# A hybrid decoder step on one core: another order for the steps of its token mixing

## The chip, the cores and the metric

The kernel runs on one core of one Trainium2 chip. The metric is the device time of one execution in microseconds (us); less is better. Three timed runs of the kernel before gave 1505.63, 1511.18 and 1495.79 us, the median is 1505.63 us.

## The reference

One inference step of a one-layer decoder, for 512 prompt tokens and 8 x 8 sample tokens (576 columns in all) with a model width of 1024, in float32. Cut to what matters:

```
x = x + 0.5 * swiglu(rmsnorm(x), ffn1)
z = rmsnorm(x) @ w_in                       # zs (RWKV), zc (conv), zq (attention), zg (gates)
y_a = rwkv7(zs)                             # 8 heads of 64: shift, decay, wkv scan, group norm
y_b = silu(layernorm(depthwise_conv31(glu(zc)))) @ w_conv_out
y_c = attention(zq, 256 memory tokens) @ w_xattn_out
g0, g1, g2 = sigmoid(zg)
x = x + (g0 * y_a + g1 * y_b + g2 * y_c) @ w_o
x = x + 0.5 * swiglu(rmsnorm(x), ffn2);  y = rmsnorm(x)
```

Beside y, the new RWKV states, shift rows, convolution tails and the memory's keys and values are outputs.

## The kernel before

Activations lie transposed, 128 channels in the partitions and 576 token columns in the free dimension, in two halves of 288. Every float32 matrix is split into a high and a low fp32r part, and a product is three matmuls (high by high, high by low, low by high). A **projection** (`proj`, line 111) loads one 128 x 1024 weight tile from HBM, splits it (ACT casts the high part at line 95, DVE subtracts the low part at line 96) and runs 8 x 3 matmuls for each half, 48 in all, at line 109, into two banks of the PSUM group `p`.

The first feed-forward layer, the token mixing and the second feed-forward layer follow one another. The mixing is what the change is about. Its steps are written down by hand in the string `PLAN` (line 28) and traced in that order by the loop at line 252:

- **A**: attention (770) to the memory, with two projections; results in `oc`.
- **P0 to P3**: preparation (866) of one pair of RWKV heads. Three projections with the token shift (`shifted`, 588) into the single tiles `k`, `r`, `v`; then a row of small passes through the PSUM group `g`: sums of squares (910), spreading of the norms (915), the products `gr` (945, 947), transposes (958 to 963).
- **I0 to I3**: inverse (1017) of the small triangular matrices of that pair, as a chain of 51 dependent DVE instructions (1045 to 1049). The data is laid out anew by way of HBM before it (1031, 1033, into the one tile `lt`) and after it (1053 to 1058, from the one tile `tt`): 14 DMAs on SP's queue.
- **J0 to J3**: joined (1060), two small rounds of matmuls that fill in the corner of the inverse.
- **B0 and B2**: the chains (966, 1109) of two pairs each, eight 64-token chunks in order, each a short sequence of PE, ACT and DVE steps, with the samples' chunk between them and `py` in group `g`; then `mixed` (974), group norm and gating of the result, for the first pair through group `c`, for the second through `g`. B0's result goes to HBM, B2's stays in SBUF for the merge.
- **G0**: the convolution's inputs (`glu`, 695), four projections. **C0**: the convolution itself (`conv`, 719), 124 DVE instructions (727 to 731), then a layer norm in three passes through group `g` (mean at 734, sums and root at 742, spreading at 746), SiLU, and the split into `cb` (751).
- **Y, X, Z**: gates, eight of each (848, 854). Y is a projection with a sigmoid and a store; X adds the attention's output projection from `oc` (12 matmuls); Z the convolution's from `cb` (12 matmuls) and adds to what X stored. The number behind the letter says how many.
- **L0**: reads the first two pairs' results back (1010).

Three things set the order in which the chip does this. First, the tile layer puts each engine's instructions into a fixed order at build time; it goes by the program's order, but takes an instruction of a later step where one of an earlier step would not be ready. Second, PSUM groups are rings: `p` has 3 banks, `g` 2 and `c` 3, and a ring is handed out in the program's order, so that a later step's `g` pass can't come before an earlier step's. The same holds for the weight tiles, so projections run strictly in the program's order: this row of projections is called the background stream below. Third, tiles that exist once (`k`, `r`, `v`, `lt`, `tt`) have to be free again. The tiles of the odd pairs and of the chains (`b21`, `b3`, with `vu`) are made when attention has given up its own.

Before the mixing's steps proper, `low_rank` (631) makes decay, mixing rate and gate for all four pairs; line 691 copies the gate's eight half tiles from PSUM.

Of the kernel before, what the change touches and what calls it, by code (L numbers as in the profile page):

```python
# [9 lines left out]
ALU = mybir.AluOpType  # L10
# [14 lines left out]
NORMED = 1  # L25

ROOMS = (8, 9, 10, 11, 12, 0, 1, 2, 3, 4, 8, 9, 10, 11, 5, 6, 7, 0, 8, 9, 10, 11)
PLAN = ("A0 P0 I0 Y3 G0 P1 J0 I1 Y3 X1 J1 B0 X3 P2 I2 Y2 X2 P3 J2 X2 I3 C0 Z2 J3 B2 Z4 L0 Z2")
PADN = 8 * 65 + 8 * 9
GRP = 11  # L30
NPROB = 36
# [18 lines left out]
class _Builder:  # L50
# [122 lines left out]
    def build(self):  # L173
        tc, a = self.tc, self.a
        with ExitStack() as st:
# [22 lines left out]
            with ExitStack() as sf:  # L198
# [17 lines left out]
                for k in range(8):  # L216
# [34 lines left out]
                    "Z": [(lambda i=i: self.gated(gp, 1, "cb", self.cb, i, 0)) for i in range(8)]}  # L251
            for step in PLAN.split():
                n = int(step[1:])
# [377 lines left out]
    def low_rank(self, zp):  # L631

        V, A, T, a, b1 = self.V, self.A, self.T, self.a, self.b1
        two = lambda name, n: zp.tile([128, 2, n], F32R, name=name)
        sub = lambda o, x, hi: V.tensor_tensor(o, x, hi.bitcast(F32), ALU.subtract)
        wh, wl, gh, gl = two("wh", 512), zp.tile([128, 512], F32R, name="wl"), two("gh", 512), zp.tile(
            [128, 512], F32R, name="gl")
        xs, lg, gs = two("xs", N), two("lg", N), zp.tile([128, N], F32R, name="gs")  # L640
        x = b1.tile([128, N], F32, name="k")
        self.shifted(12, x, b1)
        A.activation(x[:64], x[:64], AF.Tanh)
        for i in range(2):
            o, q = slice(64 * i, 64 * i + 64), slice(64 - 64 * i, 128 - 64 * i)
            A.copy(xs[o, i], x[o])
            sub(xs[q, i], x[o], xs[o, i])
        x = b1.tile([128, N], F32, name="r")
        self.shifted(13, x, b1)
        A.activation(x, x, AF.Sigmoid)  # L650
        self.split(lg[:, 0], lg[:, 1], x)
        x = b1.tile([128, N], F32, name="av")[:96]
        self.shifted(14, x, b1)
        A.activation(x, x, AF.Sigmoid)
        A.copy(gs[:96], x)
        sub(gs[32:64], x[32:64], gs[32:64])

        t = b1.tile([128, 1024], F32, name="lt")
        self.dma(t, a["wda"])
        t = t.rearrange("p (i c) -> p i c", i=2)  # L660
        A.copy(wh, t)
        for i in range(2):
            o = slice(64 * i, 64 * i + 64)
            sub(wl[o], t[o, i], wh[o, i])
        t = [b1.tile([128, PADN], F32, name=n)[:, :512] for n in ("w", "g")]
        for i in range(2):
            self.dma(t[i], a["wg"][:, 512 * i:512 * i + 512])
            A.copy(gh[:, i], t[i])
        sub(gl, t[0], gh[:, 0])
        sub(gh[64:96, 1], t[1][64:96], gh[64:96, 1])  # L670

        def products(*ops):
            for h in range(2):
                c = slice(h * H, (h + 1) * H)
                p = self.bank("g")[:, :H]
                for q, (l, r) in enumerate(ops):
                    T.matmul(p, l, r[:, c], start=q == 0, stop=q == len(ops) - 1)  # L677
                yield c, p

        for j in range(4):  # L680
            ch = slice(128 * j, 128 * j + 128)
            for i, (par, out, name) in enumerate((("w0", self.d_w, "bv"), ("a0", self.d_a, ("k", "r")[j % 2]))):
                t = b1.tile([128, N], F32, name=name, bufs=2 - i)
                o = slice(64 * i, 64 * i + 64)
                for c, p in products((wh[:, i, ch], xs[:, i]), (wl[o, ch], xs[o, i])):
                    A.activation(t[:, c], p, AF.Sigmoid, bias=self.par(par, j))
                self.store(out[j], t)
            t = b1.tile([128, N], F32, name=("av", "zt")[j % 2])
            for c, p in products((gh[:, 0, ch], lg[:, 0]), (gh[:, 0, ch], lg[:, 1]), (gl[:, ch], lg[:, 0]),
                                 (gh[:96, 1, ch], gs[:96])):  # L690
                A.copy(t[:, c], p)
            self.store(self.d_gt[j], t)


# [670 lines left out]
```

## Time and profile before

| | |
|---|---|
| timed runs | 1505.63, 1511.18, 1495.79 us |
| profiled execution, its own time | 1491.07 us |
| its span, first to last instruction | 1489.2 us |
| PE busy | 1449.4 us (97%) |
| DVE busy | 1028.1 us (69%) |
| ACT busy | 664.4 us (45%) |
| mean granted TensorE clock | 0.974 |
| mixing, from its first steps to the merge | about 430 to 1000 us from the span's start |

All times below that name a place ("at 644 us") count from the span's start. A row of the windows view gives, for a stretch from A to B: its length, then busy time and number of instructions of PE, PEld (weight loads), DVE, ACT and POOL, the granted TensorE clock, the DMA engines' share and GB/s. A row of the timeline gives start, length, engine, line, operation, tile written and tiles read, number of instructions, and in brackets the idle time before it with what ended it. A row of a source line gives the count, the shortest, median and longest duration in ns, and the first and last start. A row of the groups of instructions gives the count, the busy time in us, the mean of one in ns, and the engine's idle time before them. A PE that is called busy is not at its peak: its matmuls overlap.

### The profile page before, as it was taken

Reading aid. Unit: us, or ns where it says so; the run is one execution under the profiler, and the core shown is the slowest. Engines: PE = TensorE matmul, PEld = TensorE weight load, DVE = VectorE, ACT = ScalarE, POOL = GpSimd, SP = SyncE. Lnnn points to the kernel's source line nnn. Section 1 sums busy time; section 2 is a strip of 40 time slices with the busy share of each in tenths; the row PEclk is TensorE's granted clock in tenths of the full one; section 3 lists DMA queues with packets and bytes.
Section 4 is the critical chain, followed back from the end, with each engine's and each line's share of the span. In section 5 each row is a group of like instructions: output and inputs, shape, how many; then the busy total and the mean of one; then the engine's idle time right before and its main releaser. Section 6 shows DMA issues by size and latency. Waiting matters only on the chain.

```text
span 1489.2 us, 27301 instructions
## 1 busy us (share of the span) xinstructions
PE 1449.4 (97%) x10884; PEld 1384.6 (93%) x10884; DVE 1028.1 (69%) x2059; ACT 664.4 (45%) x1348; POOL 5.0 (0%) x22
## 2 busy tenths in 40 slices
PE   9999999999999999999999887999999999999998
PEld 9999999999988889899889786889999999999997
DVE  7976777777875629896347763348578767777775
ACT  7443444444577733534355422344444433444442
POOL 0000000000000000000000000000000000000000
PEclk9999999999999999999999877989999999999999
DMA  6222222323644143344122332227322322233221
GB/s 209 72 86 86 86 85 86 98 88 99 198 149 154 57 140 80 89 124 117 49 89 88 92 114 75 74 87 258 101 85 72 94 78 86 89 89 107 85 86 64
DMA packets 98444, 151.28 MB, mean 102 GB/s; under 512 B 43997, under 2 KB 53725, under 8 KB 98317
## 3 DMA queue, kind: packets, MB, share of 16 engines
q1 hardware_dynamic: 97740, 148.95, 32.2%
q8 instruction: 85, 1.39, 0.4%
q10 hardware_dynamic: 576, 0.59, 0.1%
q14 instruction: 43, 0.34, 0.1%
HBM read 130.03 MB, written 19.48 MB: 100 GB/s over the span
## 4 chain that ended last, share of the span: by engine, by line
PE 90%; DVE 6%; issue 1%; ACT 1%; DMA 1%; SPq 0%; DVEq 0%; POOL 0%; ACTq 0%; POOLq 0%
PE p L109 50%; PE p L384 26%; DVE pr L1045 2%; DVE tt L1047 1%; PE g L945 1%; DVE wl L96 1%; PE g L677 1%; PE c L1122 1%; PE g L1153 1%; PE c L1139 1%; PE g L137 1%; DVE cc L730 1%; PE c L1086 1%; PE g L147 1%; PE c L1132 1%
## 5 line engine op out<-in xcount | busy, mean ns | idle before, releaser
L109 PE MATMUL p<-x,wh 128*128 128x288 f32 x3136 | 653.7, 301 | 4.2 <-ACT wh L95 3.5
L109 PEld LDWEIGHTS p<-x,wh 128*128 128x128 f32 x3136 | 511.8, 191 | 12.4 <-ACT wh L95 4.2
L109 PE MATMUL p<-x,wl 128*128 128x288 f32 x1568 | 472.0, 302 | 6.8 <-DVE wl L96 6.7
L95 ACT CAST wh<-w 128x512 fp32r<-128x512 f32 (+1 forms) x354 | 210.3, 600 | 260.9 <-PE p L384 100.0
L109 PEld LDWEIGHTS p<-x,wl 128*128 128x128 f32 x1568 | 298.5, 191 | 12.9 <-DVE wl L96 8.7
L96 DVE TENSOR_TENSOR wl<-w,wh 128x512 fp32r<-128x512 f32 (+1 forms) x354 | 232.5, 662 | 109.8 <-ACT wh L95 99.5
L384 PE MATMUL p<-t,wh 128*128 128x288 f32 x1088 | 224.3, 299 | 0.0
L384 PEld LDWEIGHTS p<-t,wh 128*128 128x128 f32 x1088 | 173.9, 188 | 6.4 <-DVE t L395 6.4
L384 PE MATMUL p<-b,wh 128*128 128x288 f32 x816 | 169.7, 295 | 0.0
L384 PE MATMUL p<-t,wl 128*128 128x288 f32 x544 | 160.6, 295 | 0.0
L95 ACT CAST wh<-p 128x512 fp32r<-128x512 f32 x136 | 84.5, 621 | 155.9 <-PE p L109 117.4
L384 PEld LDWEIGHTS p<-b,wh 128*128 128x128 f32 x816 | 132.8, 188 | 0.0
L96 DVE TENSOR_TENSOR wl<-p,wh 128x512 fp32r<-128x512 f32 x136 | 93.6, 688 | 50.6 <-ACT wh L95 47.8
L384 PE MATMUL p<-b,wl 128*128 128x288 f32 x408 | 120.4, 295 | 0.0
L384 PEld LDWEIGHTS p<-t,wl 128*128 128x128 f32 x544 | 102.5, 188 | 0.0
L384 PEld LDWEIGHTS p<-b,wl 128*128 128x128 f32 x408 | 76.8, 188 | 0.0
L462 DVE SCALAR_TENSOR_TENSOR x<-p,x 128x288 f32<-128x288 f32 x128 | 57.8, 451 | 21.2 <-PE p L109 21.2
L95 ACT CAST x<-t 128x576 fp32r<-128x576 f32 (+1 forms) x60 | 36.5, 610 | 44.8 <-DVE t L466 42.2
L374 DVE TENSOR_TENSOR p<-w 128x512 f32<-128x512 f32 x68 | 46.7, 686 | 2.4 <-DMA w<-wu 2.0
L374 DVE TENSOR_TENSOR p<-p,w 128x512 f32<-128x512 f32 x68 | 46.4, 682 | 0.1
L851 ACT ACTIVATE gate<-p 128x288 f32<-128x288 f32 x48 | 19.7, 410 | 55.9 <-PE p L109 50.6
L1165 DVE SCALAR_TENSOR_TENSOR st<-c,gc,mg 64x64 f32<-64x64 f32 x56 | 15.8, 283 | 41.3 <-PE c L1143 28.9
(380 smaller groups left out, 1990.9 us busy)
## 6 DMA issues: line engine op xcount, KB each, us to landing
w<-wu SPq DMA_DIRECT2D x85, 512.0 KB
w<-win SPq DMA_DIRECT2D x44, 512.0 KB
w<-wd SPq DMA_DIRECT2D x64, 256.0 KB
w<-wd SPq DMA_DIRECT2D x16, 384.0 KB
d_mb<-gate SPq DMA_DIRECT2D x16, 288.0 KB
w<-wo SPq DMA_DIRECT2D x8, 512.0 KB
d_x<-x SPq DMA_DIRECT2D x16, 144.0 KB
d_g<-gate SPq DMA_DIRECT2D x8, 288.0 KB
```

The costliest lines, as they stand in the source:

```text
L95: self.A.copy(hi, x)
L96: self.V.tensor_tensor(lo, x, hi.bitcast(F32), ALU.subtract)
L109: self.T.matmul(p, l, x[r][:, c], start=k == 0 and i == 0, stop=k == n - 1 and i == 2)
L137: self.T.matmul(p[:, i * w:(i + 1) * w], t[:, o:o + 128], sel, start=q == 0, stop=q == len(ops) - 1)
L147: self.T.matmul(p[:, o + f - d.start:o + 128 - d.start], r[f:, i], self.con("ident")[f:, f:], start=True, stop=True)
L374: V.tensor_tensor(s, u, v, ALU.add)
L384: self.T.matmul(p, hl[l][:, c], xs[k][b][:, o], start=first and k == 0 and q == 0, stop=k == 3 and q == 2, skip_group_check=True)
L462: V.scalar_tensor_tensor(x[m][:, c], p, 0.5, x[m][:, c], ALU.mult, ALU.add)
L677: T.matmul(p, l, r[:, c], start=q == 0, stop=q == len(ops) - 1)
L851: self.A.activation(g[:, c], p, AF.Sigmoid)
L1045: V.tensor_tensor(pr, tt[:, :n, :e].unsqueeze(2).broadcast_to([np_, n, m, e]), l3[:, t:e, :e].unsqueeze(1).broadcast_to([np_, n, m, e]), A ...
L1165: V.scalar_tensor_tensor(mn[s, i, s], p, g[s], mg[s, s], ALU.mult, ALU.add)
```

## The change

The steps of the mixing are put into another order, and the eight gate copies of `low_rank` go from ACT to DVE. Nothing is computed that was not computed before.

```
-PLAN = ("A0 P0 I0 Y3 G0 P1 J0 I1 Y3 X1 J1 B0 X3 P2 I2 Y2 X2 P3 J2 X2 I3 C0 Z2 J3 B2 Z4 L0 Z2")
+PLAN = "A0 P0 I0 P1 J0 G0 Y2 I1 J1 B0 C0 X2 P2 I2 Y3 X2 P3 J2 Y3 X2 I3 X2 J3 B2 Z6 L0 Z2"
...
             for c, p in products((gh[:, 0, ch], lg[:, 0]), (gh[:, 0, ch], lg[:, 1]), (gl[:, ch], lg[:, 0]),
                                  (gh[:96, 1, ch], gs[:96])):
-                A.copy(t[:, c], p)
+                V.tensor_scalar(t[:, c], p, 1.0, None, ALU.mult)
             self.store(self.d_gt[j], t)
```

Step by step: P1 and J0 come straight behind I0, ahead of three Y and of G0. Between P1 and P2, the stream holds G0, two Y and two X instead of three Y and four X. C0 stands behind B0 and ahead of P2, instead of behind I3. Three Y and two X stand between P2 and P3, instead of two and two; three Y and four X behind P3 ahead of B2, instead of two X and the first two Z. All Z stand behind B2, six and then, behind L0, two.

## The prediction

> **What bounds the kernel now.** I read the page first, then the windows over the mixing's steps, then the source lines that begin and end each inverse, and last the timeline at the places where these are late. The page's head:
>
> ```profile
> span 1489.2 us, 27301 instructions
> PE 1449.4 (97%) x10884; PEld 1384.6 (93%) x10884; DVE 1028.1 (69%) x2059; ACT 664.4 (45%) x1348; POOL 5.0 (0%) x22
> ```
>
> PE counts as busy for 97%, but a busy PE need not be a full one, so I count matmuls by stretch. One stretch of the second feed-forward layer is the measure, the others are I0, the time up to I1, I1, B0, I2, the gap to I3, I3, the gap to B2, and B2:
>
> ```profile
> 1150.00:1200.00 50.00, 50.00 (x377) 49.81 (x376) 35.55 (x66) 20.62 (x39) 0.00 (x0) 1.00 0.27 85
> ...
> 551.00:586.00 35.00, 32.45 (x225) 31.29 (x225) 28.44 (x72) 10.13 (x25) 0.00 (x0) 0.90 0.37 120
> 586.00:644.00 58.00, 56.34 (x451) 53.23 (x450) 52.77 (x97) 27.79 (x58) 0.00 (x0) 0.97 0.35 94
> 644.00:685.00 41.00, 40.73 (x305) 40.16 (x303) 41.00 (x101) 12.06 (x25) 0.00 (x0) 1.00 0.42 131
> 703.00:760.00 57.00, 57.00 (x539) 46.06 (x535) 19.20 (x45) 19.83 (x65) 0.00 (x0) 0.97 0.14 37
> 816.00:853.00 37.00, 33.72 (x219) 30.68 (x217) 30.44 (x78) 14.21 (x27) 0.00 (x0) 0.91 0.28 87
> 853.00:873.00 20.00, 14.53 (x136) 14.09 (x136) 5.32 (x11) 8.73 (x15) 0.00 (x0) 0.82 0.44 104
> 873.00:902.00 29.00, 22.94 (x149) 22.21 (x150) 27.20 (x68) 6.80 (x15) 0.00 (x0) 0.83 0.31 102
> 902.00:917.00 15.00, 7.98 (x97) 7.62 (x96) 1.67 (x3) 1.99 (x6) 0.00 (x0) 0.77 0.50 125
> 917.00:985.00 68.00, 67.54 (x534) 54.61 (x532) 24.26 (x56) 23.69 (x71) 0.00 (x0) 0.83 0.19 50
> ```
>
> The measure: 377 matmuls in 50 us, 0.133 us each, 6.4 us for a projection, 8.0 us for an X or Z with its 12 more. In the mixing PE falls short of that from 816 to 917, where it idles 21.8 us of 101 (3.3, 5.5, 6.1 and 7.0) and the clock is granted at 0.77 to 0.91. DVE is full in I1 (41.00 of 41). So neither engine bounds the whole stage. What orders it is a chain: P0's products, I0, I1, B0, P2's products, I2, I3, J3, B2, merge. Where each inverse begins and ends (first and last start of its reductions):
>
> ```profile
> L1047 DVE TENSOR_REDUCE tt<-pr x20: 159/389/535, 551.2 to 585.4; 108x2 f32<-108x6 f32 x1, 108x4 f32<-108x20 f32 x1, 108x6 f32<-108x42 f32 x1, 108x6 f32<-108x54 f32 x1
> ...
> L1047 DVE TENSOR_REDUCE tt<-pr x20: 149/403/550, 644.8 to 685.3; 108x2 f32<-108x6 f32 x1, 108x4 f32<-108x20 f32 x1, 108x6 f32<-108x42 f32 x1, 108x6 f32<-108x54 f32 x1
> ...
> L1047 DVE TENSOR_REDUCE tt<-pr x20: 155/385/526, 816.0 to 852.0; 108x2 f32<-108x6 f32 x1, 108x4 f32<-108x20 f32 x1, 108x6 f32<-108x42 f32 x1, 108x6 f32<-108x54 f32 x1
> ...
> L1047 DVE TENSOR_REDUCE tt<-pr x20: 159/381/527, 873.6 to 901.0; 108x2 f32<-108x6 f32 x1, 108x4 f32<-108x20 f32 x1, 108x6 f32<-108x42 f32 x1, 108x6 f32<-108x54 f32 x1
> ```
>
> The same 20 rounds take 34, 41, 36 and 27 us, by what DVE does between them. Work that is in the background stream does not set the end as long as the chain is longer; the change counts by what it does to this chain.
>
> **Part 1: P1 ahead of three Y and of G0.** I1 begins 59 us behind the end of I0 (585.4 to 644.8). The timeline says why:
>
> ```profile
> 557.32 0.58 ACT L963 COPY vu<-g 64x512 f32<-64x512 f32 x1
> ...
> 599.64 0.78 ACT L907 ACTIVATE u<-k,pv 128x576 f32<-128x576 f32 x1 [2.60 <-DVE k L605]
> ...
> 629.91 0.29 DVE L947 TENSOR_TENSOR gr<-g,cst 128x128 f32<-128x128 f32 x1 [0.37 <-PE g L945]
> ...
> 642.82 0.09 DVE L1034 MEMSET lt<- 108x32 f32 x1
> ```
>
> P1's first small pass starts at 599.6, since its key projection stands behind Y3 and G0 (seven projections, 45 us). Its last product is masked at 630.2, and the new layout by HBM has landed in `lt` at 642.8, 13 us later. In the new order P1's three projections take the place of the three Y. The first moment at which the `g` ring lets P1 in is when P0's value transposes leave it, at 557.3 and just behind: they wait for `vu`, that is for attention's end, before and after. P1 then needs at most the 30.6 us that it took (599.6 to 630.2), so its products are ready by 588, about when I0 gives up `lt`. I1 would begin at 603 to 606 instead of 644, some 40 us earlier. That is the upper bound. The lower one is DVE's load: from 551 to 685 it is busy 28.4 + 52.8 + 41.0 = 122 of 134 us, so 12 us are all that squeezing wins, if everything that it did by 685 still stands ahead of I1's end. It does not. Between 551 and I1's end five fewer projections are split (G0, Y2, X2, P2 instead of G0, P1, Y3, X4 and two of P2), and the convolution is taken only where the inverse leaves a gap:
>
> ```profile
> L730 DVE SCALAR_TENSOR_TENSOR cc<-up,pv,cc x60: 712/742/773, 580.9 to 683.3; 128x512 f32<-128x512 f32 x60
> ...
> 552.01 0.90 SPq L85 DMA_DIRECT2D w<-win  x2
> ...
> 852.57 0.86 SPq L1053 DMA_DIRECT2D s<-tt  x1
> ```
>
> Its inputs come from G0, which stays where it was in time (its first weights are loaded at 552, when SP is through with attention's loads), so it again starts near 581; what is not done by I1's end falls into B0, where DVE is busy 19 of 57 us. I take 28 us, nearer the upper bound: **-28 (-40 to -12)**. J0 moves with it and is off the chain. I1's 14 DMAs now stand on SP's queue ahead of the weights of X2 and P2 rather than of X and P2's last; an issue takes up to 0.86 us, 12 us for all. The stream's weights lie a tile ahead and hide this, so I cost it at nothing; uncovered, it would delay the stream by 12 us and the chain not at all. P2's projections also run earlier, but P2 must wait for B0 in any case.
>
> **Part 2: C0 behind B0.** The convolution's norm needs the `g` ring three times, and P2's first pass now stands behind it. Before, it stood behind P3's last transposes:
>
> ```profile
> 774.93 0.82 DVE L992 TENSOR_TENSOR u<-u,g 128x512 f32<-128x512 f32 x2 [0.48 <-PE g L147]
> ...
> 776.22 1.17 PE L137 MATMUL g<-cst,u 128*128 128x2 f32 x10
> ...
> 791.75 1.71 PE L945 MATMUL g<-ra,kb 64*128 64x128 f32 x16
> ...
> 830.04 0.26 ACT L963 COPY vu<-g 64x128 f32<-64x128 f32 x1 [0.24 <-PE g L962]
> ...
> L734 ACT ACTIVATE sg<-g x2: 411/411/411, 835.5 to 836.5; 128x288 f32<-128x288 f32 x2
> ...
> L746 DVE TENSOR_TENSOR cc<-cc,g x4: 223/456/692, 850.1 to 852.6; 128x512 f32<-128x512 f32 x2, 128x64 f32<-128x64 f32 x2
> ```
>
> The last convolution step was done at 684, the mean was copied at 835.5: the ring held it for 150 us. It is ready long before B0 ends, so in the new order its three passes run right behind `mixed`'s last reading of `g` (774.9 before) and hold P2's sums (776.2, with its products 15.5 us later at 791.8) for the time from the mean to the spreading. That was 17.3 us (835.5 to 852.8), in the middle of I2. Without I2 in the way it is shorter: the instructions of it that are quoted here come to 4.2 us (two copies of 0.4, and 1.7, 1.5 and 0.2 in the rows of part 3). **+13 (+5 to +18)** on the chain. The SiLU and the split behind it hold no ring.
>
> **Part 3: C0 out of I2.** There it cost:
>
> ```profile
> L746 DVE TENSOR_TENSOR cc<-cc,g 128x512 f32<-128x512 f32 (+1 forms) x4 | 1.7, 456 | 2.8 <-PE g L147 2.8
> L737 DVE TENSOR_TENSOR cc<-cc,sg 128x576 f32<-128x576 f32 x2 | 1.5, 749 | 0.0
> ...
> L743 DVE RECIPROCAL rt<-rt 128x5 f32<-128x5 f32 x1 | 0.2, 190 | 0.9 <-ACT rt L742 0.9
> ```
>
> 3.4 us of DVE and 3.7 us of waiting at the head of DVE's queue, with the inverse behind it: 7 us of the 9 by which I2 is longer than I3. With one more for the casts of `cb` between I2 and I3: **-8 (-12 to 0)**.
>
> **Part 4: eight copies from ACT to DVE.**
>
> ```profile
> L691 ACT COPY zt<-g 128x288 f32<-128x288 f32 x4 | 1.6, 395 | 0.2
> ...
> L858 DVE TENSOR_TENSOR gate<-p,gate 128x288 f32<-128x288 f32 x32 | 14.6, 455 | 20.6 <-ACT gate L851 10.4 <-PE p L109 9.6 <-ACT vu L1140 0.6
> ...
> 450.00:500.00 50.00, 49.92 (x315) 41.93 (x314) 24.93 (x62) 38.60 (x92) 0.00 (x0) 1.00 0.35 117
> ```
>
> No row shows this form on DVE; the nearest reads two operands of the same size from PSUM and SBUF in 0.455 us. 8 x 0.395 = 3.2 us leave ACT, which is busy 38.6 of 50, and up to 3.6 us come to DVE, which is busy 24.9 and hides them; without that cover they would cost the 3.6. **-1 (-3 to +1)**.
>
> **Part 5: the stream behind P2's products.** The stream stops at P3's third projection until P2 has given up `k`. From there 3 Y, 4 X and 8 Z follow with half of P3, 6.4 + 19 + 32 + 64 = 121 us; before, from 792 on, it was two of P3, 2 X and 8 Z, 93 us. The 28 us more go into the 21.8 us of idle shown above, the rest lengthens I2 to B2 or runs over. Matmuls behind idle time also start slow. **+5 (0 to +12)**. Ahead of that PE stands still for some 25 us between B0 and P2's products, which the chain does not feel.
>
> Sum: -28 + 13 - 8 - 1 + 5 = **-19 us**; bounds -40 + 5 - 12 - 3 + 0 = -50 and -12 + 18 + 0 + 1 + 12 = +19. On the profiled execution, 1491.1 us with 1489.2 of span and 2 around it, that makes 1472. That execution lies 1.0% under the median of the timed runs, 1505.6, and below their lowest, 1495.8; I subtract the same 19 from the median: **1486 us**.
>
> **A rule of the Trainium skill.** What a cold PE costs shows at B2's first chunk against a later one:
>
> ```profile
> 910.00:920.00 10.00, 6.13 (x81) 5.63 (x82) 0.64 (x1) 2.51 (x7) 0.00 (x0) 0.50 0.41 116
> ...
> 917.17 1.11 PE L1122 MATMUL c<-vu,gr 64*64 64x64 f32 x8
> ...
> 934.51 0.68 PE L1122 MATMUL c<-vu,gr 64*64 64x64 f32 x8
> ```
>
> Granted 0.50 there, eight small matmuls took 1.11 instead of 0.68 us. A chunk has about three such groups, so a chain of eight chunks that stays cold costs 8 x 3 x 0.43 = 10 us. The Trainium skill, "TensorE: Matmul & The Clock Gate", section "Why this matters for your kernels", says to leave no idle gap over about 3 us between bursts, since the clock then falls to half; by that rule the stand-still speaks against this change, and the trace agrees with it behind 902 to 917.
>
> **The rivals.**
> - *More (1462).* The convolution slides behind I1 for the most part: -40 in part 1, +5 in part 2, 0 in part 5, the rest as above, -44. For it: DVE is two thirds idle in B0. Against it: before, 60 of 60 steps were squeezed in by 684. Chance 0.17.
> - *Given back (1503).* The second half is then bound by PE: 28 us more in the stream do not fit, because idle PE time there is in-order waiting and not lack of work. Part 5 is then 21, the 28 less some 7 that fit, and 16 of the 19 go. For it: B2 holds only 534 matmuls in 68 us though PE never stops. Chance 0.21.
> - *Cold (1497).* PE stands still through B0 and stays at half rate: +10 on the sum. Against it: the stream still holds Y3, X2 and two of P3 when B0 starts. Chance 0.10.
> - *Slower (1526).* DVE is the bound up to I1's end, the convolution's steps lie between those of I0 and I1 both, and I1 ends where it did; then C0's 17 us on the `g` ring and 8 for part 5, less 5 for parts 3 and 4, remain: +20. It decides once I1 ends later than 676, where part 1 no longer covers the other parts, 13 - 8 - 1 + 5 = 9. For it: DVE at 41.00 of 41 in I1. Chance 0.12.
> - That the order does not change what runs when: not likely, since the stream follows the text.
>
> **How the numbers follow.** My forecast, -10 to -32 us, has 0.40. Three runs differ by 1% here, so 1% (15 us) is what can be told from no change. Of the forecast's 0.40, 0.36 lie beyond 15 us; with 0.17 that makes 0.53 faster. The rest of it, given back and cold make 0.35 the same, 0.12 slower. The range 1458 to 1516 leaves out the ends of the bounds, the far part of *more* and that of *slower*; the likeliest case alone has 1474 to 1496.
>
> **What would show it.** Right: I1's first reduction near 605 and its last near 657; L734 right behind `mixed`'s last L992, and P2's sums (L137, then L910) some 13 us behind it; I2 under 30 us; B2's end near 965; the idle PE time moved from 816-917 to the stretch ahead of P2's products. Wrong: I1 ending past 676, a stretch from P2's products to B2's end longer than the 194 us of before, or much of the stream left behind B2.

## The result, and the profile after

The changed kernel is slower. Its median is 1546.12 us (1539.98 to 1553.46, four runs) against 1502.62 us of the kernel before on the same chip; the ratio is 1.0289, with a 95% interval of 1.0213 to 1.0364, some 43 us. The forecast of 1486 and its range up to 1516 both miss. The profiled execution took 1539.98 us, its span is 49.0 us longer than before. A trace shows a single execution, and those of one kernel differ by about 1% (the trace of the kernel before is of one of 1491.07 us, 12 us under that median), so that a difference of some 10 us between places in two traces says little by itself. The head of the page:

```profile
span 1538.2 us, 27287 instructions
...
PE 1471.3 (96%) x10884; PEld 1403.3 (91%) x10884; DVE 1032.9 (67%) x2067; ACT 662.2 (43%) x1341; POOL 5.0 (0%) x22
...
PE   9999999999999999189999999999999999999997
```

The last line is the page's row of slices for PE: 40 slices of 38.5 us, in tenths. Before, no slice stood below 7; now there is a 1 at 615 to 654. The stretches of the mixing, in the columns of the prediction (I0; up to I1; two pieces of I1; B0; P2's products up to I2; I2; the gap to I3; I3; B2; behind B2):

```profile
548.00:593.00 45.00, 42.14 (x251) 38.05 (x251) 33.46 (x89) 18.79 (x39) 0.00 (x0) 0.81 0.24 68
593.00:620.00 27.00, 25.88 (x239) 25.12 (x237) 25.41 (x51) 9.56 (x21) 0.00 (x0) 1.00 0.57 121
620.00:656.00 36.00, 1.13 (x6) 0.75 (x5) 36.00 (x87) 0.13 (x1) 0.00 (x0) 0.53 0.01 4
656.00:667.00 11.00, 10.79 (x69) 10.56 (x68) 11.00 (x18) 2.62 (x6) 0.00 (x0) 0.84 0.19 60
...
682.00:774.00 92.00, 91.54 (x627) 76.30 (x626) 30.26 (x69) 34.38 (x99) 0.00 (x0) 0.73 0.16 43
...
805.00:829.00 24.00, 23.58 (x180) 22.12 (x180) 13.31 (x22) 9.74 (x22) 0.00 (x0) 1.00 0.34 104
829.00:861.00 32.00, 27.12 (x182) 25.17 (x181) 30.63 (x79) 13.20 (x29) 0.00 (x0) 0.89 0.14 47
861.00:874.00 13.00, 13.00 (x66) 11.44 (x66) 4.26 (x8) 5.21 (x10) 0.00 (x0) 0.61 0.46 82
874.00:899.00 25.00, 25.00 (x222) 24.49 (x222) 5.41 (x10) 8.80 (x21) 0.00 (x0) 0.93 0.37 109
899.00:927.00 28.00, 26.76 (x198) 26.11 (x197) 25.73 (x67) 7.11 (x15) 0.00 (x0) 1.00 0.35 107
...
941.00:1005.00 64.00, 64.00 (x545) 52.53 (x543) 24.26 (x57) 21.85 (x69) 0.00 (x0) 0.89 0.23 65
1005.00:1050.00 45.00, 41.93 (x302) 40.92 (x301) 22.99 (x43) 22.60 (x41) 0.00 (x0) 0.96 0.67 216
```

The third row matters most: for 36 us PE does 1.1 us of work, with DVE at 36.00 of 36. Next comes B0 (682 to 774): 92 us for 627 matmuls at a granted clock of 0.73. And behind B2, where before 116 matmuls were left (985 to 1002), stand 302 in 45 us. The inverses' reductions:

```profile
L1047 DVE TENSOR_REDUCE tt<-pr x20: 159/380/517, 548.2 to 593.5; 108x2 f32<-108x6 f32 x1, 108x4 f32<-108x20 f32 x1, 108x6 f32<-108x42 f32 x1, 108x6 f32<-108x54 f32 x1
...
L1047 DVE TENSOR_REDUCE tt<-pr x20: 149/385/524, 620.2 to 666.2; 108x2 f32<-108x6 f32 x1, 108x4 f32<-108x20 f32 x1, 108x6 f32<-108x42 f32 x1, 108x6 f32<-108x54 f32 x1
...
L1047 DVE TENSOR_REDUCE tt<-pr x20: 159/392/534, 828.8 to 860.4; 108x2 f32<-108x6 f32 x1, 108x4 f32<-108x20 f32 x1, 108x6 f32<-108x42 f32 x1, 108x6 f32<-108x54 f32 x1
...
L1047 DVE TENSOR_REDUCE tt<-pr x20: 159/386/524, 899.5 to 927.1; 108x2 f32<-108x6 f32 x1, 108x4 f32<-108x20 f32 x1, 108x6 f32<-108x42 f32 x1, 108x6 f32<-108x54 f32 x1
```

What PE waits for at 620 is in the timeline (the first rows are the start of the stall, the last its end):

```profile
618.68 1.45 ACT L95 CAST wh<-w 128x512 fp32r<-128x512 f32 x3
...
620.30 0.74 DVE L730 SCALAR_TENSOR_TENSOR cc<-up,pv,cc 128x512 f32<-128x512 f32 x1
620.42 0.29 PE L109 MATMUL p<-oc0l,wh 128*128 128x288 f32 x1
620.96 0.21 DVE L1049 SCALAR_TENSOR_TENSOR tt<-tt,sub 108x1 f32<-108x1 f32 x1
621.09 0.74 DVE L730 SCALAR_TENSOR_TENSOR cc<-up,pv,cc 128x512 f32<-128x512 f32 x1
621.75 0.18 DVE L1045 TENSOR_TENSOR pr<-tt,lt 108x20 f32<-108x20 f32 x1
621.86 0.74 DVE L730 SCALAR_TENSOR_TENSOR cc<-up,pv,cc 128x512 f32<-128x512 f32 x1
...
654.47 0.44 DVE L1047 TENSOR_REDUCE tt<-pr 108x10 f32<-108x280 f32 x1
654.82 0.68 DVE L96 TENSOR_TENSOR wl<-w,wh 128x512 fp32r<-128x512 f32 x1
...
655.55 0.61 PE L109 MATMUL p<-x,wl 128*128 128x288 f32 x1 [34.84 <-DVE wl L96]
```

The next projection's weights are there, and ACT has cast their high part by 620. The low part is a DVE subtraction (L96, 0.68 us), whose inputs are ready from then on. But DVE works through its list in order, and on that list a convolution step stands between any two steps of I1, for 34 us, before the subtraction comes. So the convolution does not fill gaps here; it has become work that others queue behind. At the other end of the mixing, the last gate addition of a Z, the second pair's last product of `mixed` and the merge's first product, first before, then after:

```profile
L862 DVE TENSOR_TENSOR gate<-gate,gm x8: 746/750/758, 861.2 to 1001.5; 128x576 f32<-128x576 f32 x8
...
L997 DVE TENSOR_TENSOR u<-gt,u x2: 698/722/746, 993.1 to 1000.9; 128x576 f32<-128x576 f32 x2
...
L1227 DVE TENSOR_TENSOR gate<-p,gate x16: 444/450/458, 1006.4 to 1028.3; 128x288 f32<-128x288 f32 x16
```

```profile
L862 DVE TENSOR_TENSOR gate<-gate,gm x8: 749/752/758, 932.3 to 1049.8; 128x576 f32<-128x576 f32 x8
...
L997 DVE TENSOR_TENSOR u<-gt,u x2: 752/756/759, 1013.7 to 1022.8; 128x576 f32<-128x576 f32 x2
...
L1227 DVE TENSOR_TENSOR gate<-p,gate x16: 449/457/458, 1051.2 to 1075.3; 128x288 f32<-128x288 f32 x16
```

Before, the chain (1000.9) and the background stream (1001.5) ended level. Now the chain ends 22 us later and the stream 48 us later, and the merge waits for the stream. Place by place:

| place (start, us) | before | after | difference |
|---|---|---|---|
| I1, first and last reduction | 644.8, 685.3 | 620.2, 666.2 | -25, -19 |
| B0's first product (L1122) | 703.7 | 682.1 | -22 |
| `mixed`'s last use of `g` (L992) | 775.5 | 773.1 | -2 |
| P2's first product (L945) | 791.7 | 805.0 | +13 |
| I2, last reduction | 852.0 | 860.4 | +8 |
| I3, last reduction | 901.0 | 927.1 | +26 |
| last product of `mixed` (L997) | 1000.9 | 1022.8 | +22 |
| last Z (L862) | 1001.5 | 1049.8 | +48 |
| the merge's first product (L1227) | 1006.4 | 1051.2 | +45 |
| end of the span | 1489.2 | 1538.2 | +49 |

### The profile page after: what moved, and what is told of

It reads as the page before. It is cut to its first block, busy times and chain, and to the rows that moved or that the text cites. A ratio compares the mean times of both kernels' runs of the same rounds, so it can differ in the third digit from the quotient of the medians.

```text
span 1538.2 us, 27287 instructions
## 1 busy us (share of the span) xinstructions
PE 1471.3 (96%) x10884; PEld 1403.3 (91%) x10884; DVE 1032.9 (67%) x2067; ACT 662.2 (43%) x1341; POOL 5.0 (0%) x22
## 3 DMA queue, kind: packets, MB, share of 16 engines
q1 hardware_dynamic: 97740, 148.95, 31.6%
## 4 chain that ended last, share of the span: by engine, by line
PE 51%; DVE 3%; ACT 1%; DMA 1%; issue 1%; SPq 0%; DVEq 0%; ACTq 0%
PE p L109 29%; PE p L384 13%; PE c L1122 1%; DVE pr L1045 1%; PE c L1139 1%; PE g L1153 1%; PE c L1086 1%; PE g L945 1%; PE c L1132 1%; DVE tt L1047 1%; PE c L1106 1%; PE c L1143 0%; PE g L1151 0%; PE c L1201 0%; DVE x L1242 0%
## 5 line engine op out<-in xcount | busy, mean ns | idle before, releaser
L109 PE MATMUL p<-x,wh 128*128 128x288 f32 x3136 | 660.4, 303 | 5.4 <-ACT wh L95 4.7
L96 DVE TENSOR_TENSOR wl<-w,wh 128x512 fp32r<-128x512 f32 (+1 forms) x354 | 232.4, 662 | 153.5 <-ACT wh L95 145.0
L96 DVE TENSOR_TENSOR wl<-p,wh 128x512 fp32r<-128x512 f32 x136 | 93.6, 688 | 50.5 <-ACT wh L95 47.7
L730 DVE SCALAR_TENSOR_TENSOR cc<-up,pv,cc 128x512 f32<-128x512 f32 x60 | 43.8, 743 | 0.9 <-DVE lt L1034 0.9
```

Source lines behind the costliest of these rows:

```text
L96: self.V.tensor_tensor(lo, x, hi.bitcast(F32), ALU.subtract)
L109: self.T.matmul(p, l, x[r][:, c], start=k == 0 and i == 0, stop=k == n - 1 and i == 2)
L730: V.scalar_tensor_tensor(c[:, :SEQ], up[:, k:k + SEQ], w, c[:, :SEQ], ALU.mult, ALU.add)
```

## Experiments on the stall

My theory: the convolution belongs to C0, and C0 now stands ahead of X2 and P2 in the text. The build goes by the text's order, so it puts the convolution's steps ahead of the weight splits of X2 and P2, and PE starves. Rivals: C0's three passes through group `g` ahead of P2, the thinner stream behind P1, the Z behind B2, the copies.

**C0 put back behind I3** (`c0_late`), all else as changed:

```
-... I1 J1 B0 C0 X2 P2 I2 Y3 X2 P3 J2 Y3 X2 I3 X2 J3 B2 Z6 L0 Z2
+... I1 J1 B0 X2 P2 I2 Y3 X2 P3 J2 Y3 X2 I3 C0 X2 J3 B2 Z6 L0 Z2
```

> The changed kernel with C0 put back behind I3 (and so behind X2, P2 and all that follows), everything else as changed. Theory (the convolution, standing in the text ahead of X2, is built into DVE's fixed order ahead of X2's weight split, and PE waits for that split): the stall of 34.8 us at 620 to 655 falls below 5 us, B0 runs at a full clock, P2's products come some 25 us earlier than in the changed kernel, and the time falls by 30 to 45 us, to a ratio of 0.995 to 1.01 of the kernel before. Rival (moving P1 ahead has thinned the stream, and PE starves there whatever DVE does): the stall stays above 20 us and the ratio above 1.02. Rival (six Z behind B2 are the loss): the stall goes but the ratio stays above 1.02, since the tail behind B2 stays.

Measured: ratio 1.0024 (0.9986 to 1.0061). The row of PE's waits for weight splits, 600 to 700 (total, times, longest):

```profile
PE p L109 <- DVE wl L96: 3.0, 2, 2.3
```

In the changed kernel the same row reads:

```profile
PE p L109 <- DVE wl L96: 35.5, 3, 34.8
```

The stall is gone, and 1.0289 - 1.0024 = 2.65%, 40 us, come back, although the six Z still stand behind B2. Both rivals of that expectation fall. I1 ends and B0 begins where they did in the changed kernel (664.5 and 680.7 against 666.2 and 682.1), but P2's first product comes at 771.1 instead of 805.0.

**X2 ahead of C0** (`x2_first`): only these two are exchanged.

```
-... B0 C0 X2 P2 ...
+... B0 X2 C0 P2 ...
```

> The changed kernel with two steps exchanged: X2 ahead of C0, C0 still ahead of P2. Theory (order of the text between the convolution and the next weight split): the first 16 us of the stall are filled by X2, P2's projections then meet the same convolution, so a stall of 15 to 22 us stays at about 640 to 660 and the time falls by 10 to 20 us against the changed kernel. Rival (C0's three passes through group g ahead of P2 are the loss): those stay where they are, the time falls by less than 5 us. Rival (the stream is too thin there): the stall keeps its length and only moves, time within 5 us.

Measured: 1.0211 (1.0134 to 1.0287), 12 us less than the changed kernel.

```profile
PE p L109 <- DVE wl L96: 26.0, 2, 24.9
```

The time falls as expected and the stall less than expected: 24.9, not 15 to 22. X2's weights now pass, P2's are caught.

**One tap** (`one_tap`): 30 of the convolution's 31 taps are left out, C0 stays where the change put it.

```
-            for k in range(31):
+            for k in range(1):
```

> The changed kernel with one tap of the convolution instead of 31 (30 of 31 taps are left out, some 45 us of DVE work and 120 instructions); C0 stays behind B0 with its three passes through group g. Theory (the convolution's DVE instructions, built ahead of the weight split, starve PE): the stall at 620 to 655 falls below 8 us and the time by 35 to 50 us against the changed kernel, ratio 0.985 to 1.005 of the kernel before. Rival (C0's passes through group g ahead of P2, or P1's new place, are the loss): ratio stays above 1.015.

Measured: 0.9938 (0.9896 to 0.998), 53 us less than the changed kernel.

```profile
PE p L109 <- DVE wl L96: 2.4, 2, 1.8
```

With the DVE work gone the stall is gone, though C0's passes through `g` are still ahead of P2 and hold its sums until 758.7, 14.5 us behind `mixed`'s last use of `g`. So it is the convolution's own steps, and not the passes, that cost the 40 us.

**C0 between P2 and I2** (`c0_mid`), and the same with two Z ahead of J3 (`c0_mid_z`):

```
-... B0 C0 X2 P2 I2 ... I3 X2 J3 B2 Z6 L0 Z2
+... B0 X2 P2 C0 I2 ... I3 X2 J3 B2 Z6 L0 Z2      (c0_mid)
+... B0 X2 P2 C0 I2 ... I3 X2 Z2 J3 B2 Z4 L0 Z2   (c0_mid_z)
```

> The changed kernel with C0 between P2 and I2, so behind the weight splits of X2 and P2 in the text, and out of I2, I3 and B2. Theory (only C0's place ahead of the splits costs, and without it the stream on PE sets the end): no stall over 5 us between 600 and 700, P2's sums right behind mixed as in c0_late, I2 not longer than in c0_late, but the merge begins within 6 us of c0_late's; ratio 0.99 to 1.005 of the kernel before. Rival (C0 anywhere near P2 delays the chain): ratio 1.01 or more.

> As c0_mid, with two of the six Z ahead of J3 and B2 in the text, where the kernel before has two. Theory (the stream sets the end, its order is the same, only its rank against B2 on PE changes): the last mixed comes 5 to 15 us later, the last Z 0 to 8 us earlier, ratio 0.004 to 0.0 below c0_mid's. Rival (six Z behind B2 are a loss of their own): 10 us less than c0_mid or better.

Measured: 1.0171 (1.0119 to 1.0223) and 1.0153 (1.0095 to 1.0211). I was wrong on the first: I had taken X2 and P2 for the only splits in danger. The row of `c0_mid`:

```profile
PE p L109 <- DVE wl L96: 15.8, 4, 14.3
```

Now the splits of Y3, next in the text, are caught, for 14.3 us at 659 to 674. In each of the three places of C0 it is the next projections of the text that wait. The Z's place makes no difference that can be told from none.

Taken together, the longest wait for a split against the ratio, in the order of the changed kernel with only C0 moved: 2.3 us, 1.0024; 14.3, 1.0171; 24.9, 1.0211; 34.8, 1.0289.

**The kernel before with C0 alone moved**, behind B0 (`c0_only`) and between P2 and I2 (`before_c0_mid`):

```
-... J1 B0 X3 P2 I2 ... I3 C0 Z2 ...
+... J1 B0 C0 X3 P2 I2 ... I3 Z2 ...   (c0_only)
+... J1 B0 X3 P2 C0 I2 ... I3 Z2 ...   (before_c0_mid)
```

> The kernel before with one step moved: C0 straight behind B0, ahead of X3. Theory: the convolution then stands ahead of X3's weight splits but behind those of the second Y3 and of X1, so PE is fed through most of I1 and stands still for at most 10 to 20 us near its end; C0's norm passes hold group g ahead of P2 besides. Ratio 1.00 to 1.02. Rival (C0's place is harmless, the loss comes from P1): ratio 0.99 to 1.00 and no stall over 5 us between 640 and 720.

> The kernel before with one step moved: C0 between P2 and I2. It prices C0's removal from I2 without the stall and without P1's move. The prediction's terms: 8 us less in I2, and nothing on group g ahead of P2, so ratio 0.993 to 0.997 if the chain sets the end; 0.998 to 1.003 if what the chain gains is lost to the stream.

Measured: 1.0054 (1.0026 to 1.0083), with a longest wait of 8.9 us, below the 10 to 20 expected; and 0.9979 (0.9939 to 1.0019), no difference that can be told. In the old order a second Y3 and X1 stand ahead of B0 and keep PE fed while the convolution runs, so C0's early place costs 8 us instead of 40. It takes both, P1 ahead and C0 ahead, to starve PE for long: with P1 ahead and fewer gates, nine projections (P1, G0 and two Y) lie between I0 and B0 instead of fourteen (Y3, G0, P1, Y3 and X1). That the number of projections is what makes the difference is argued, not shown.

**The copies back on ACT**, in the changed kernel (`act_copy`), in `c0_mid` (`c0_mid_act`) and in `c0_late` (`c0_late_act`), and onto DVE in the kernel before (`before_dve`):

```
-                V.tensor_scalar(t[:, c], p, 1.0, None, ALU.mult)
+                A.copy(t[:, c], p)
```

> The changed kernel with the eight gate copies of the low-rank step put back on ACT. Theory: the copies take 0.455 us each on DVE instead of 0.395 on ACT, lie where DVE is half idle, and matter by under 2 us: ratio within 0.004 of the changed kernel's. Rival (3.6 us more on DVE ahead of the mixing shift everything behind): 3 to 5 us less than the changed kernel.

> As c0_mid, with the copies of line 691 on ACT. Theory (copies on DVE cost 0.06 us more each and lie beside other work): within 0.003 of c0_mid. Rival (they hold up the start of the mixing, as the 8 us between the changed kernel and act_copy suggest): 0.004 to 0.006 below c0_mid.

> The run with C0 put back behind I3 (c0_late), with the copies of line 691 on ACT as in the kernel before. Theory (copies cost under 2 us): ratio within 0.002 of c0_late's 1.0024. Rival (the copies on DVE cost 5 to 8 us, as in both pairs so far, 1.0289 to 1.0236 and 1.0171 to 1.0118): ratio 0.996 to 0.999.

> The kernel before with the copies of line 691 on DVE and nothing else. Theory (under 2 us): ratio 0.999 to 1.001. Rival (5 to 8 us): ratio 1.003 to 1.006.

Measured: 1.0236 (1.0188 to 1.0285) against 1.0289; 1.0118 (1.0069 to 1.0168) against 1.0171; 0.9954 (0.9921 to 0.9987) against 1.0024; and 1.0013 (0.9979 to 1.0046). In each pair the two intervals overlap, but all three kernels of the new order come out 0.5 to 0.7%, 8 to 11 us, higher with the copies on DVE, and the old order shows nothing that can be told. The eight copies themselves are cheap:

```profile
L691 DVE TENSOR_SCALAR av<-g x4: 447/458/458, 450.9 to 463.4; 128x288 f32<-128x288 f32 x4
L691 DVE TENSOR_SCALAR zt<-g x4: 451/458/458, 455.7 to 470.2; 128x288 f32<-128x288 f32 x4
```

That is 0.06 us more each than on ACT. So the 8 us are not their duration. In all three pairs the first gate behind G0 comes 6 to 10 us later with the copies on DVE (606.2, 606.1 and 605.0 us against 596.6, 596.3 and 598.7), and I0 begins 8 to 11 us earlier (548.2, 550.9 and 550.4 against 559.1, 558.8 and 561.2). In the first pair the stall is longer besides (34.8 against 30.2 us). So it looks as if the copies change the order in which the build lays out what follows, with the chain earlier and the stream later. That this is what costs the time is argued, not shown.

## Experiments on what the earlier inverses are worth

Without the stall, I1 still ends some 20 us earlier than before (664.5 in `c0_late`), and yet the time is that of the kernel before. Where does that go?

**P1 alone moved, in the kernel before** (`p1_only`):

```
-A0 P0 I0 Y3 G0 P1 J0 I1 ...
+A0 P0 I0 P1 J0 Y3 G0 I1 ...
```

> The kernel before with one step moved: P1 and J0 straight behind I0, ahead of Y3 and G0; the copies on ACT, C0 behind I3, the rest as before. Theory A (what the prediction took for granted: the chain of inverses sets the end): I1 begins some 30 us earlier, and so do B0, P2 and B2; the time falls by 20 to 30 us, ratio 0.98 to 0.987. Theory B (the end of the mixing is set by the background stream on PE, which has as much work as before): the inverses and the last mixed come 15 to 30 us earlier, but the last Z and the merge begin within 8 us of where they did, ratio 0.993 to 1.005.

Measured: 1.0036 (0.9998 to 1.0073): theory B's ratio. The move that carried my forecast is worth nothing by itself. Whether the chain ended earlier can't be read here: the trace is of an execution of 1526.41 us, 17 us above the median of 1509.89.

**Two Y projections left out**, in `c0_late` (`six_y`) and in the kernel before (`before_six_y`); their gates are stored from the two Y before them:

```
+    def gate_two(self, pool, i):
+        if i < 6:
+            g = self.gate(pool, 0, i)
+            self.store(self.d_g0[i], g)
+            if i > 3:
+                self.store(self.d_g0[i + 2], g)
```

> The run with C0 put back behind I3 (c0_late), and the last two of the eight Y projections left out (their gates are stored from the two Y before them, 12.8 us of PE and their weight splits less). In c0_late the last mixed was done at 984.2 and the last Z at 1005.1. Theory B (the stream sets the end there): the merge begins 10 to 16 us earlier, ratio 0.99 to 0.995. Theory A (the chain sets it): less than 4 us.

> The kernel before with the last two of the eight Y projections left out in the same way (their gates are stored from the two Y before them). In the kernel before the last mixed was done at 1001.6 and the last Z at 1002.3, level. If the chain sets the end: less than 4 us, ratio 0.997 to 1.0. If the stream sets it: 10 to 16 us less, ratio 0.989 to 0.993. If the two are tied to each other, since both share PE and its clock: 4 to 10 us.

Measured: 0.9899 (0.9854 to 0.9945), 19 us less than `c0_late` for 12.8 us of projections; and 1.001 (0.9975 to 1.0045), nothing. So a shorter stream gains in the new order, where it ended last, and nothing in the old one, where the two ended level. The size is not explained: 19 us are more than the stream was shortened by, and in the two traces the merge begins only 5.8 us earlier (999.9 against 1005.7). The two ends in `c0_late`:

```profile
L862 DVE TENSOR_TENSOR gate<-gate,gm x8: 748/752/759, 874.8 to 1004.4; 128x576 f32<-128x576 f32 x8
...
L997 DVE TENSOR_TENSOR u<-gt,u x2: 758/758/759, 974.3 to 983.4; 128x576 f32<-128x576 f32 x2
```

The chain ends at 983.4, 17.5 us earlier than before, and then the merge waits for a Z that ends at 1004.4, 3 us later than before. The gain is there and is stopped at the next bound. In `c0_late_act`, the same order with the copies on ACT, the gap is smaller: the chain's last product is at 1004.6 and the last Z at 1010.9. `before_six_y` adds how closely the two are tied. Its last Z is done at 968, 44 us ahead of the chain's last product, and what remains of the chain runs alone, with 174 matmuls in 40 us and half the clock:

```profile
970.00:1010.00 40.00, 34.58 (x174) 27.63 (x173) 10.81 (x25) 12.76 (x33) 0.00 (x0) 0.51 0.12 30
```

Its last product of `mixed` comes at 1012.4, 11.5 us later than before. It looks as if what was taken out of the stream came back as a slower chain; but this execution took 12 us more than the one in the trace of the kernel before (1503.24 against 1491.07 us), while the medians are level, so that the 11.5 us may be no more than the two executions' difference.

**Idle work for PE** (`c0_late_warm`, `before_warm`): 24 matmuls without use in each of J1 and J3, so that the clock would not fall there.

```
+                if j % 2 and c % 2:
+                    busy()
...
+        for _ in range(8 * (j % 2)):
+            busy()
```

> The run with C0 put back behind I3 (c0_late), with 24 idle-work matmuls of 128 x 128 by 288 put among the small rounds of J1 and J3 each; their products are not used, and they are 3.2 us of PE each time. In c0_late the clock was granted at 0.50 for most of 890 to 935, straight behind J3's rounds, while the last mixed was 21 us earlier than the last Z. Theory (the gain of the earlier chain is lost to PE's half clock, which begins at the thin rounds of J): the clock is above 0.85 from J3 to 30 us behind it, the last Z comes 8 to 20 us earlier, ratio 0.989 to 0.998. Rival (the half clock comes from B2's own thin groups): clock and time as in c0_late or 3 to 6 us more, ratio 1.002 to 1.007.

> The kernel before with the same idle-work matmuls in J1 and J3. Before, the clock was 1.00 from 670 to 750 and 0.50 for 15 us from 910. Theory: half of these 15 us is won back at most, less the 6.4 us of PE work: ratio 0.997 to 1.004. Rival (half clock comes from the thin groups of the chains): ratio 1.002 to 1.007.

Measured: 1.0151 (1.0106 to 1.0197) and 1.0212 (1.0148 to 1.0275). Neither theory's time came: these kernels lose 19 and 32 us for 6.4 us of added work. The clock did not stay up either. In `c0_late_warm` it is 0.50 from 920 to 940, at J3's rounds and behind them, as the rival had it; there and in `before_warm` it falls while the idle matmuls run, one of which takes 0.40 us up to 916.5 and 702.1, and 0.61 from 917.1 and 705.3 on. The stretch from 700 to 760, in which B0 begins (703.7 and 712.0), in the kernel before, then in `before_warm`:

```profile
700.00:760.00 60.00, 60.00 (x588) 48.69 (x587) 19.20 (x45) 21.30 (x69) 0.00 (x0) 0.97 0.13 35
```

```profile
700.00:760.00 60.00, 60.00 (x479) 48.13 (x479) 13.34 (x34) 17.09 (x54) 0.00 (x0) 0.83 0.12 33
```

Why is open; the idle matmuls also take a bank of group `c`, which the chains use, and change the order that the build makes.

**One tap in the old order** (`before_one_tap`), to stand beside `one_tap`; again 30 of 31 taps are left out:

> The kernel before with one tap of the convolution instead of 31 (30 of 31 taps left out), to stand beside one_tap, which was at 0.9938 with the changed order. Theory (without the stall, the new order is worth nothing, since what the earlier inverses win is used up on PE): ratio 0.988 to 0.998, within 0.004 of one_tap's. Rival (the new order is worth its 19 us once the convolution is out of the way): ratio 1.00 to 1.01. Rival (the old order is the better one even then): below 0.988.

Measured: 1.0099 (1.0061 to 1.0138), against 0.9938 in the new order. So with the convolution out of the way the new order (with its copies) is better than the old one by 1.6%, 24 us, close to the 19 that I had forecast. Of these, though, only 0.6% are a gain on the whole kernel before; the other 1.0% is that the old order gets slower with 43 us less of DVE work (985.2 us busy against 1028.1). The second theory's range holds that ratio, but it gives no reason for it, and it stays open. So this pair doesn't show by itself what the new order is worth.

**More stream at the start of B0** (`fill_b0`): `c0_late_act`, with one Y and one X ahead of J1.

```
-A0 P0 I0 P1 J0 G0 Y2 I1 J1 B0 X2 P2 I2 Y3 X2 P3 J2 Y3 X2 I3 C0 X2 J3 B2 Z6 L0 Z2
+A0 P0 I0 P1 J0 G0 Y2 I1 Y1 X1 J1 B0 X2 P2 I2 Y2 X2 P3 J2 Y3 X1 I3 C0 X2 J3 B2 Z6 L0 Z2
```

> The run with C0 behind I3 and the copies on ACT (c0_late_act, 0.9954), with one Y and one X moved ahead of J1 and B0, one Y from between P2 and P3, one X from ahead of I3 and one more X between J3's neighbours exchanged accordingly: the stream then has two more projections to fill PE at the end of I1 and the start of B0. Theory (half clock in B0 takes the gain; more stream there keeps it full): clock above 0.9 from 680 to 750, mixed's last reading of group g some 10 us earlier than c0_late_act's 773.4, ratio 0.988 to 0.994. Rival (the half clock comes with the chains' thin groups whatever lies beside them): clock and time as in c0_late_act, ratio 0.993 to 0.999.

Measured: 0.9907 (0.9872 to 0.9942), median 1480.06 us against 1498.42 of the kernel before. It beats both kernels, the one before by 0.93%, 14 us. The 60 us in which B0 begins (686.5 and 685.6), in `c0_late_act`, then here:

```profile
680.00:740.00 60.00, 59.81 (x534) 50.50 (x533) 17.92 (x45) 19.62 (x60) 0.00 (x0) 0.86 0.21 63
```

```profile
680.00:740.00 60.00, 60.00 (x553) 49.11 (x551) 18.96 (x46) 19.95 (x61) 0.00 (x0) 0.91 0.21 64
```

The clock is higher, though over 680 to 750 it is 0.88 (0.84 in `c0_late_act`) and not the 0.9 that I expected. `mixed`'s last use of `g` comes at 765.9 instead of 773.2, 7 us earlier and not 10, and the ends are at 980.3 (chain) and 987.0 (last Z), instead of 1004.6 and 1010.9:

```profile
L862 DVE TENSOR_TENSOR gate<-gate,gm x8: 746/752/758, 872.2 to 987.0; 128x576 f32<-128x576 f32 x8
...
L997 DVE TENSOR_TENSOR u<-gt,u x2: 752/754/757, 971.2 to 980.3; 128x576 f32<-128x576 f32 x2
```

Chain and stream both end earlier than before here (1000.9 and 1001.5), so that a gain arrives. Its cause is argued, not shown: the two traces are of executions 24 us apart (1477.09 and 1501.31 us), the ratios 0.5%, 7 us, so that most of these differences in place and clock may be the executions'. That it is better than `c0_late_act` (0.9921 to 0.9987) is likely and not sure: the intervals overlap.

## Why the prediction was wrong

**The step that failed** is in part 1: "the convolution is taken only where the inverse leaves a gap". I read that from the kernel before, where C0 stood behind everything in the text, and kept it when part 2 moved C0 ahead of X2 and P2. I costed C0's move by group `g` alone and put the place of its 124 DVE instructions at nothing, without asking what they would now be ahead of. In the changed order, 34 us of steps of the convolution and of I1 stood ahead of a split of 0.68 us, and PE stood still for 34.8 us. The convolution's 60 large steps (L730) ran from 594.6 to 653.1 and were all done ahead of I1's end, where the prediction had them begin near 581 and partly fall into B0; put back, in `c0_late`, they are spread from 591.9 to 679.0. `c0_late`, `one_tap` and the row of waits show it; it is worth 40 us of the 43. The rival *slower* had the convolution's steps between those of I1, but saw the loss in a late I1; I1 came 19 us earlier, and the weight splits were late.

**Part 1** had the right sign and too large a size for the chain: I1 ended 19 us earlier, not 28, inside the bounds (12 to 40). I0 itself took 45 us instead of 34; steps of P1 (L947) and of G0 (L711) that wait for PE now stand between its own on DVE, and ten convolution steps stood ahead of I1's first:

```profile
585.95 0.29 DVE L947 TENSOR_TENSOR gr<-g,cst 128x128 f32<-128x128 f32 x1 [1.35 <-PE g L945]
...
589.94 0.45 DVE L711 SCALAR_TENSOR_TENSOR up<-p,pv,sg 128x224 f32<-128x224 f32 x1 [1.35 <-PE p L109]
...
611.14 6.71 DVE L730 SCALAR_TENSOR_TENSOR cc<-up,pv,cc 128x512 f32<-128x512 f32 x10
617.83 0.09 DVE L1034 MEMSET lt<- 108x32 f32 x1
```

Then none of it reached P2. B0 began 22 us earlier and ended 2 us earlier, 91 us long instead of 72, at a clock of 0.73 instead of 0.98. This is the rival *cold* in another place than I had put it: I gave it 10 us and a chance of 0.10. That the stall made B0 slow is not shown. Without it, B0 took 75 us at 0.95 in `c0_late`, but 87 us at 0.78 in `c0_late_act`, and in `before_dve`, which has the old order and a ratio of 1.0013, 90 us at 0.77.

**"Work that is in the background stream does not set the end as long as the chain is longer"** is the other step that failed: the chain was not longer. In the kernel before the two ended level, the stream even 0.6 us later (1001.5 against 1000.9), and the prediction quotes neither end. So a shorter stream gains nothing there (`before_six_y`), P1's move alone gains nothing (`p1_only`), and in `c0_late` a chain shortened by 17.5 us shows nothing. This is the rival *given back*, and `six_y` speaks for it.

**Part 2** was right: P2's sums began 13.6 us behind `mixed`'s last use of `g` (773.1 to 786.7), with C0's passes between, where before it was 0.7. P2's first product came 32 us behind it, before 16, so 16 us for the predicted 13 (5 to 18). **Part 3**: I2 took 31.6 us instead of 36.0, 4 us for the predicted 8. **Part 4**: the duration was within bounds, the effect on the order was not in the list at all. **Part 5**, 0 to 12 us predicted, was the second large miss (in its working, the "half of P3" at 6.4 us is one of three projections; the sum is unaffected): P3's products came late behind three Y and two X of a stream that had stood still for 35 us, so that I3 began 39 us behind I2's end instead of 22, and 27 us of Z were left behind the chain's end.

Of my signs, "I1 ending past 676" did not show, since I1 ended at 666; the two others did: P2's products to B2's end took 200 us, not 194, and much of the stream was left behind B2. "Ahead of that PE stands still for some 25 us between B0 and P2's products, which the chain does not feel" was wrong in place and in effect: it stood still for 35 us, during I1, and the stream, which now sets the end, felt it.

What stays open: why the clock falls to half in B0 in some executions and orders and not in others, why idle matmuls made it worse, why `six_y` gains more than it leaves out, and why the kernel before loses 1% without its convolution.

## What to carry to other kernels

Where a build fixes each engine's order from the order of the text, filler work is safe as filler while it stands behind the urgent work in the text; moved forward, every instruction of it can become something that short urgent work (here a weight split of 0.7 us) queues behind. When a step is moved, list its instructions on every engine, and what stands behind them there, not only the ring it holds. And before shortening a chain, look up when the next bound ends: here the stream ended 0.6 us behind the chain already.

## What the runs showed of the hardware

A PE that the profile counts as busy throughout can stay at half clock. In `c0_late`, during B2:

```profile
910.00:930.00 20.00, 20.00 (x112) 15.30 (x110) 5.01 (x12) 2.71 (x10) 0.00 (x0) 0.50 0.27 75
```

It is 20.00 of 20, with 112 matmuls where a dense stretch of the prediction's measure has 151 in that time, and the clock stays at 0.50. The Trainium skill, "TensorE: Matmul & The Clock Gate", section "Why this matters for your kernels", has the clock fall when PE is left idle between bursts. The stall agrees: 0.53 granted over 620 to 656, with PE at 1.13 of 36. In B2 this row shows no idle time at all, and the longest pause of PE that the trace shows from 880 to 930 is 1.22 us, with the clock at 1.00 from 880 to 890 and at 0.53 from 890 to 900. So a PE that the profile calls busy is not enough here to keep the clock up. It can't be seen here whether the thin work keeps the clock low or the low clock makes the work look thin.
